# Narrow attention products filled to 128 rows of the array, with doubled low parts or zeros

## The chip, the cores and the metric

The kernel runs on one core of one Trainium2 chip. The metric is the device time of one execution in microseconds (us), the median of several runs. TensorE multiplies matrices, VectorE, ScalarE and GpSimd do the work by element, and one queue of SyncE (SP) issues all the DMAs of this kernel.

## The reference, cut to what matters

One inference step of a hybrid encoder trunk with two layers, all in 32-bit floats. A layer normalises its input, projects it, and runs three branches side by side: differential attention (DA: 4 heads, each with two maps of 64 features), a state-space scan (SSM), and stick-breaking attention (SB: 8 heads of 64 features). Their outputs are projected and added to the input, and a gated FFN with a short convolution follows.

```python
def diff_attn_block(q, k, v, q_pos, q_chunk, k_pos, k_chunk, rel_table, lam):
    ...
    s = jnp.einsum('bqhmd,bkhmd->bmhqk', q, k).astype(jnp.float32) * scale
    s = jnp.where(mask, s + bias[None, None].astype(jnp.float32), NEG_INF)
    p = jax.nn.softmax(s, axis=-1)
    p = p[:, 0] - lam * p[:, 1]
    return jnp.einsum('bhqk,bkhv->bqhv', p.astype(v.dtype), v)

def stick_breaking_block(q, k, v, q_pos, k_pos):
    z = jnp.einsum('bqhd,bkhd->bhqk', q, k).astype(jnp.float32) * (SB_HEAD_DIM ** -0.5)
    mask = k_pos[None, :] < q_pos[:, None]
    log_keep = jnp.where(mask, jax.nn.log_sigmoid(-z), 0.0)
    tail = lax.cumsum(log_keep, axis=3, reverse=True) - log_keep
    w = jnp.where(mask, jnp.exp(jax.nn.log_sigmoid(z) + tail), 0.0)
    return jnp.einsum('bhqk,bkhd->bqhd', w.astype(v.dtype), v)
```

There are 16 meta tokens and 512 prompt tokens in one sequence, and 8 sampled sequences of 16 new tokens that also attend to 512 cached ones each.

## The kernel before

All activations stand feature-major, with 656 columns: 16 meta, 512 prompt, 8 x 16 sampled (`NP` is 528). The dense products split each operand into a high part, rounded to the format fp32r, and a low part, the rest of it. A product is then three of fp32r, each one pass of TensorE; a product of whole 32-bit floats is two passes.

A layer runs SSM input and scan, then `da` for two pairs of heads (s = 0, 1), then `sb` for two groups of heads, and then the output projection `w_out` and the FFN. The in-projection of the next pair (`qkv_in`, issued with a priority offset of 400) and the parts of `w_out` that are ready are the dense work that TensorE does between the steps of an attention. The order of all instructions on each engine is fixed when the kernel is built, by a planner that simulates the engines and takes instructions by priority; the queues then run in that order.

The products that this case is about have fewer than 128 rows (the contracted index, on the partitions) because a head has 64 features, or because a block of keys has 16:

- `da_prompt`, scores. `stacked` puts the high part of a head's queries on the head's own 64 rows and the low part on the other 64 (`qs`), and the high part of its keys on both (`kd`). One product of 128 rows gives high by high plus low by high. The low part of the keys (`kl`) has only the head's own 64 rows, and a second product adds high by low from these:

```python
                    self.mm(ps, qs, kd[m][:, a:b], True, False)
                    self.mm(ps, qs[hs], kl[m][hs, a:b], False, True)
```

  The first block of queries (j = 0) doesn't use these, but whole floats on 64 rows (`qk,qk` in the profile).
- `sb_prompt`, scores: the same with keys and queries exchanged, `ks` by `qd` and then by `ql`.
- `da_prompt`, values. Prompt queries of block j see 128(j+1) + 16 keys. The weights are transposed by blocks of 128 keys (tile `pt`), the last 16 keys as a block of their own, and the product with these has 16 rows (`pv<-pt,vt 16*128`).
- `da_sample_values` and `sb_sample`: the new keys of four sampled sequences, 64 of them, are one half of the rows of `vt[:, 5]`; the product with the weights (`pts` or `nwt`) has 64 rows. In a DA group, products of 32 columns of the array (cached values, `kv` by `pts`) come right after it.

The tile `kv` holds 512 KB of cached keys or values, with four buffers in the pool of each branch.

Of the kernel before, what the change touches and what calls it, by code (L numbers as in the profile page):

```python
# [10 lines left out]
F32 = mybir.dt.float32  # L11
F32R = mybir.dt.float32r
# [6 lines left out]
# Columns of every feature-major tile: 16 meta tokens, 512 prompt tokens, then 8 sequences x 16 tokens.  # L19
# [15 lines left out]
# columns of the packed per-layer parameters  # L35
P_NM, P_NF, P_SUB, P_CW, P_CB, P_D, P_SN, P_FW, P_FB = 0, 8, 16, 17, 49, 57, 61, 65, 131
P_LQ, P_DTB, P_AL, P_N = 153, 157, 158, 159
# columns of the packed constants
# [3 lines left out]
class Bank:  # L42
    """Products that add into regions of one PSUM bank: the first clears its flags, the others are issued after it,
    so that each region starts from its first product."""
# [13 lines left out]
class Trunk:  # L58
# [33 lines left out]
    def act(self, out, in_, func, **kw):  # L92
        """ScalarE activation, the tables switched only between phases: all that use one set are issued before
        any of the next phase"""
        nc, tc = self.nc, self.tc
        mode = "silu_and_others" if func == AF.Silu else "natural_log_exp_and_others"
        nosync = mybir.DependencyInfo(mybir.DependencyClass.NoSync, mybir.DependencyReason.DATA)
        if mode != self.mode:
            self.gate = nc.scalar.preload_act_table_set(mode).ins
            for i in self.phase:  # L100
                tc.add_manual_dep(self.gate, i.name, nosync, reason="activation tables")
            self.mode, self.phase = mode, []
        i = nc.scalar.activation(out=out, in_=in_, func=func, **kw).ins  # L103
        tc.add_manual_dep(i, self.gate.name, nosync, reason="activation tables")
        self.phase.append(i)

    # ---------------------------------------------------------------- dense products
# [12 lines left out]
    def dense(self, wap, rhs, evac, cols=128, c0=0, w=None):  # L120
        """rhs: list of (hi, lo) tiles [128, T]; evac(columns, psum) reads the product of one half of them."""
# [18 lines left out]
    # ---------------------------------------------------------------- norms  # L140
    def x_first(self, g, pool):
        """x * g of the input and its norm"""
# [37 lines left out]
    def rstd_from(self, ss, n, out):  # L180
        """ss: sums of squares in PSUM, by half; out = (ss / n + eps) ** -0.5"""
# [5 lines left out]
    def ones_sum(self, *srcs, parts=None, tags=None):  # L187
        """sums over the partitions, on every partition, by half; with room for them, from the parts of src"""
# [19 lines left out]
    def scaled(self, out, scale=None):  # L208
        """evac writing psum * rstd (* scale) to out [*, T]"""
# [11 lines left out]
    def ext_evac(self, ext, hist):  # L221
        """evac writing psum * rstd with `hist` columns of room before the prompt and before each sequence"""
# [18 lines left out]
    def conv_silu(self, pool, ext, hist, wcol, bcol, out):  # L241
        """out[:, :T] = silu(depthwise causal conv of ext + b)"""
# [13 lines left out]
    # ---------------------------------------------------------------- the residual  # L256
# [5 lines left out]
    def x_load(self, src, pool=None, late=0):  # L262
        """the residual, in a pool of its own or in the room of the normalised one's high parts"""
# [8 lines left out]
    # ---------------------------------------------------------------- set-up  # L272
    def setup(self, ctx):
# [21 lines left out]
        # sums over the rows with the same place in blocks of 32  # L295
# [25 lines left out]
    def bias_tables(self, oneh, tab):  # L321
        """relative-position bias by (row, key) for the prompt, the sampled sequences and the meta rows"""
        nc, tc, D = self.nc, self.tc, self.D
        with tc.tile_pool(name="bp", bufs=1, reuse_waits="tile") as bp:
# [11 lines left out]
            # 128 copies of each head's row, so that a row's distance can differ from the next one's by one  # L336
# [23 lines left out]
    # ---------------------------------------------------------------- mixing-branch outputs  # L360
    def mix_pair(self, pool, tag, bufs):
        """two tiles of the output projection's operand"""
# [3 lines left out]
    def w_out(self, l, k0, pairs, nf_cols=None, offset=0, xpool=None):  # L366
        """x += the group's rows of the output projection; the last group moves x to xpool and prepares the FFN norm"""
# [27 lines left out]
    # ---------------------------------------------------------------- SSM branch  # L395
    def ssm_in(self, l, sp, spa):
# [7 lines left out]
        # dt rows  # L404
# [28 lines left out]
        # what is left of the decay to the end of each chunk  # L433
# [20 lines left out]
    def dt_in(self, l, pool, u):  # L454
        """the in-projection's tile of 8 columns, the parts of its weights side by side"""
# [27 lines left out]
    def ssd(self, l, sp, spb):  # L483
# [6 lines left out]
        for j, (t0, n) in enumerate(SCHUNK):  # L490
            sample = j == 5
            tsl = slice(t0, t0 + n)
            # token-major copies
# [7 lines left out]
            # C B^T, by group, sources on the partitions  # L501
# [70 lines left out]
            else:  # L572
                # the cached states' part: sequences on blocks of 32 rows, four at a time
# [34 lines left out]
                # what the sequences add to their states: two on each 32 rows, one of them masked  # L608
# [20 lines left out]
    def ssm_z(self, l, sp):  # L629
        """silu(z) = z / (1 + exp(-z)); the exponent is bounded where the quotient has long been 0"""  # L630
# [13 lines left out]
    def ssm_out(self, l):  # L644
        """gate, normalise per group; returns the two mix pairs"""
# [24 lines left out]
    # ---------------------------------------------------------------- attention inputs  # L670
    def qkv_in(self, l, v, outs_k, pool, offset=0):
        """four in_proj tiles, two of q (scaled) and two of k, and two more by token for the values"""
# [16 lines left out]
    def token_rstd(self):  # L689
        """the norm's factors by token: blocks of tokens on the partitions"""  # L690
# [6 lines left out]
        # 32 tokens from the last ones of the prompt  # L697
# [5 lines left out]
    def values(self, wap, vt):  # L703
        """two tiles of the in-projection, tokens on the partitions"""
        nc = self.nc
        w = [self.weights(wap[i], 4, 256, raw=True) for i in range(2)]
        for b0 in (4, 0, 2):
            ps = self.til(self.pmm, [128, 512], tag="mm")
            if b0 == 4:
                # the few tokens of block 4: four groups of products on blocks of 32 columns of the array  # L710
# [13 lines left out]
            with self.prio(-100):  # L724
                for b in (b0, b0 + 1):
                    if b == 4:
                        # the sums of the groups, until their own sum takes their place
# [13 lines left out]
    def q_blocks(self, pool, q, meta, tag):  # L741
        """queries as [128 (h2, d), (b, h2, t)], zero off the diagonal of h2"""
# [11 lines left out]
    # ---------------------------------------------------------------- differential attention  # L754
    def lam_cols(self, l, lam_init):
# [7 lines left out]
        # -(e1 - e2 + lam_init)  # L763
# [4 lines left out]
    def softmax_half(self, pool, rows, pss, tab, st, m):  # L768
        """exp(scores + bias - max) for map m, the scores in one or two pieces; the sums go to st"""
        nc = self.nc  # L770
        e = self.til(pool, [128, 576], tag="e", bufs=5)[:rows]
        c, mx = 0, BIG
# [10 lines left out]
        return e  # L783

    def softmax_mix(self, rows, es, st):
        """E0 / sum0 - lam E1 / sum1"""
# [7 lines left out]
    def stacked(self, pool, t, cols, tags, bufs, h, lo=None):  # L794
        """head h of a pair's tile t as operand parts on 128 rows: (high, low) on the head's own rows and on the
        others, or with `lo` (high, high), the low parts going to lo's rows of the head"""
# [7 lines left out]
        else:  # L804
            nc.gpsimd.tensor_copy(o[oth], t[own, cols])
            nc.vector.tensor_sub(lo[own], t[own, cols], o[own].bitcast(F32))
        return o

    def da_prompt(self, h, j, A, kd, kl, tb, oh, dap):
# [8 lines left out]
        for m in range(2):  # L818
# [3 lines left out]
            for a, b in zip(cuts, cuts[1:]):  # L822
                ps = self.sc()[:, : b - a]
                if j:
                    self.mm(ps, qs, kd[m][:, a:b], True, False)
                    self.mm(ps, qs[hs], kl[m][hs, a:b], False, True)
# [3 lines left out]
            es.append(self.softmax_half(dap, 128, pss, tab, st, m))  # L830
        p = self.softmax_mix(128, es, st)
        pt = self.til(dap, [128, 5, 128], tag="pt", bufs=3)
        ps = self.til(self.p1, [128, 512], tag="tp")
        for b in range(j + 1):
            self.tr(ps[:, 128 * b : 128 * b + 128], p[:, 128 * b : 128 * b + 128], 128)
        c0 = 128 * ((j + 1) % 4)
        pe = (ps if j < 3 else self.sc())[:16, c0 : c0 + 128]
        self.tr(pe, p[:, nk - 16 : nk], 128)
        nc.scalar.copy(pt[:16, j + 1, :], pe)
        nc.scalar.copy(pt[:, : j + 1, :].rearrange("p b c -> p (b c)"), ps[:, : 128 * (j + 1)])  # L840
        pv = self.til(self.p1, [128, 512], tag="pv")[:, :128]
        for b in range(j + 1):
            self.mm(pv, vt[:, b, 128 * h : 128 * h + 128], pt[:, b, :], b == 0, False)
        self.mm(pv, vt[:16, j + 1, 128 * h : 128 * h + 128], pt[:16, j + 1, :], False, True)
        nc.scalar.copy(oh[:, t0 : t0 + 128], pv)

    def da_sample_scores(self, l, s, g, m, A, qb, tb, st, dap):
        """rows (b, h2, t) of four sequences, map m: cached keys, then the 64 new ones"""
        nc = self.nc
        ps, pn = self.sc(), self.sc()[:, :64]  # L850
        for i2 in range(2):
            kt = self.til(dap, [128, 2, PAST], tag="kv", bufs=4)
# [14 lines left out]
    def da_sample_probs(self, g, p, dap):  # L867
# [8 lines left out]
        nc.vector.tensor_copy(pt[64 * g : 64 * g + 64, 4, :], pn)  # L876
        return pt

    def da_sample_values(self, l, s, g, A, pt, oh, dap):
        """values of four sequences: rows (b, h2, t), columns (h2, value)"""  # L880
        nc = self.nc
        rg = slice(64 * g, 64 * g + 64)
        pv = self.til(self.p1, [128, 512], tag="pv")[:, :256]
        bank = Bank(self)
        bank.mm(pv, pt[rg, 4, :], A["vt"][rg, 5, :])
        for j in range(4):
            vv = self.til(dap, [128, 4, 256], tag="kv", bufs=4)
# [14 lines left out]
    def da(self, l, s, A, dap, xpool):  # L902
# [6 lines left out]
        # meta rows  # L909
# [18 lines left out]
        # prompt rows of head g, with the sampled rows of four sequences  # L928
        es, st, pr = [None] * 2, [None] * 2, [None] * 2
        kl = [self.til(dap, [128, NP], F32R, tag="kl", bufs=2) for _ in range(2)]  # L930
        for u in range(8):
            h, j = u // 4, u % 4
            if u % 4 == 0:
                kd = [self.stacked(dap, k[m], slice(0, NP), ("kd", NP), 4, u // 4, kl[m]) for m in range(2)]
# [10 lines left out]
        # head norm  # L945
# [11 lines left out]
    # ---------------------------------------------------------------- stick-breaking attention  # L957
    def softplus(self, z, sp):
        """sp = softplus(z) for z in PSUM"""
# [6 lines left out]
    def sb(self, l, s, A, sbp, qk):  # L966
        """the results take the room of the pair's queries and keys in pool qk"""
# [4 lines left out]
        # sampled sequences: rows are (b, h2, t) of four sequences, columns (pair, four sequences, (h2, d))  # L972
# [7 lines left out]
    def sb_prompt(self, pr, A, pair, qk, sbp, sample):  # L980
        """two heads; weights by (key, query); the blocks of keys go from the last to the first"""
# [6 lines left out]
        # the last queries, zero off the diagonal of the heads  # L988
# [5 lines left out]
        ql = self.til(sbp, [128, NP], F32R, tag="ql", bufs=1)  # L994
        qd = [self.stacked(sbp, q, slice(0, NP), ("qd", NP), 4, h, ql) for h in range(2)]
# [445 lines left out]
```

## Time and profile before

| | us |
|---|---|
| median of 3 runs (2157.46 to 2159.97) | 2157.52 |
| span of the profiled execution | 2148.2 |
| what lies around the span, by the median | 9.3 |
| TensorE busy | 2115.9 |
| VectorE busy | 1323.8 |
| ScalarE busy | 876.7 |
| GpSimd busy | 296.6 |

The profile shows one execution, of which the span goes from the first to the last instruction; its own time is taken as the median, so that 9.3 us lie around the span. Matmuls are pipelined, and their recorded durations overlap: what a product costs is the distance from its start to the start of the next one. In the rows, `64*128 64x272` is a product with 64 rows and 128 columns of the array in use, that streams 272 columns; `PE` is TensorE, `DVE` VectorE, `ACT` ScalarE, `POOL` GpSimd, `SPq` the DMA queue. Line 87 is the helper through which nearly all products go, so tiles tell them apart.

### The profile page before, as it was taken

To read this page: it belongs to the slowest core of one execution; us is meant where nothing else is said; L and a number is where in the kernel's file an instruction comes from. 1 tells how busy PE (TensorE), PEld (TensorE's weight loads), DVE (VectorE), ACT (ScalarE), POOL (GpSimd) and SP (SyncE) were. 2 spreads that over 40 slices of the span, in tenths; PEclk is the share of its full clock that TensorE was granted. 3 is DMA by queue.
4 is the path that set the end of the run, shared out by engine and by line. 5 is a ranking of instruction groups with operands and counts; after the bars stand their busy time and mean duration, and the time that the engine had idled before them with its cause. 6 is when DMAs were issued, how large, how long until landed. Compare 5 with 4: busy or idle time off the path is not lost. (4 is left out here: it accounts for less than half of the span.)

```text
span 2148.2 us, 36738 instructions
## 1 busy us (share of the span) xinstructions
PE 2115.9 (98%) x14704; PEld 1937.8 (90%) x14704; DVE 1323.8 (62%) x2524; ACT 876.7 (41%) x1696; POOL 296.6 (14%) x586
## 2 busy tenths in 40 slices
PE   8999999999999999999999999999999999999998
PEld 6989888877899999999999888788778999999997
DVE  7897644677775544545468975547777655454544
ACT  3535444565542322223345354436555423132224
POOL 4241000222120000000123300002122100000002
PEclk9999999999999999999999999999999999999999
DMA  5535443453222222222324354336332222222222
GB/s 181 166 95 183 149 153 121 155 197 115 70 73 79 69 69 79 65 84 64 109 91 139 92 195 159 129 123 222 126 131 63 69 79 67 78 73 72 79 67 93
DMA packets 94500, 237.61 MB, mean 111 GB/s; under 512 B 12213, under 2 KB 31669, under 8 KB 94329
## 3 DMA queue, kind: packets, MB, share of 16 engines
q1 hardware_dynamic: 94328, 235.26, 34.5%
q8 instruction: 116, 1.90, 0.4%
q14 instruction: 56, 0.45, 0.1%
HBM read 212.06 MB, written 24.50 MB: 110 GB/s over the span
## 5 line engine op out<-in xcount | busy, mean ns | idle before, releaser
L87 PE MATMUL sc<-xh,whi 128*128 128x328 f32 (+1 forms) x1664 | 521.5, 314 | 3.8 <-ACT whi L115 3.4
L87 PE MATMUL sc<-xl,whi 128*128 128x328 f32 (+1 forms) x1664 | 520.7, 313 | 2.6 <-DVE xl L150 1.9
L87 PE MATMUL sc<-xh,wlo 128*128 128x328 f32 (+1 forms) x1664 | 518.7, 312 | 0.0
L115 ACT CAST whi<-wst 128x1024 fp32r<-128x1024 f32 (+2 forms) x241 | 237.9, 987 | 613.1 <-issue 310.6
L116 DVE TENSOR_TENSOR wlo<-wst,whi 128x1024 fp32r<-128x1024 f32 (+2 forms) x241 | 285.2, 1184 | 80.4 <-ACT whi L115 76.9
L87 PEld LDWEIGHTS sc<-xh,whi 128*128 128x128 f32 x1664 | 313.6, 189 | 5.7 <-ACT whi L115 4.6
L87 PEld LDWEIGHTS sc<-xl,whi 128*128 128x128 f32 x1664 | 314.3, 189 | 4.7 <-DVE xl L150 3.0
L87 PEld LDWEIGHTS sc<-xh,wlo 128*128 128x128 f32 x1664 | 314.6, 189 | 0.8 <-DVE wlo L116 0.4
L87 PE MATMUL mm<-xh,wlo 128*128 128x328 f32 x640 | 207.0, 323 | 0.0
L87 PE MATMUL mm<-xh,whi 128*128 128x328 f32 x640 | 205.0, 320 | 0.0
L87 PE MATMUL mm<-xl,whi 128*128 128x328 f32 x640 | 204.0, 319 | 0.0
L87 PE MATMUL sc<-ah,wlo 128*128 128x328 f32 (+2 forms) x634 | 197.4, 312 | 0.0
L87 PE MATMUL sc<-al,whi 128*128 128x328 f32 (+2 forms) x634 | 197.4, 311 | 0.0
L87 PE MATMUL sc<-ah,whi 128*128 128x328 f32 (+2 forms) x634 | 197.3, 311 | 0.0
L1200 DVE TENSOR_TENSOR x<-sc,x 128x328 f32<-128x328 f32 (+1 forms) x112 | 55.7, 497 | 147.4 <-PE sc L87 147.4
L87 PEld LDWEIGHTS mm<-xh,wlo 128*128 128x128 f32 x640 | 121.3, 190 | 9.8 <-issue 6.9
L87 PEld LDWEIGHTS mm<-xl,whi 128*128 128x128 f32 x640 | 121.3, 189 | 3.6 <-issue 2.2
L87 PEld LDWEIGHTS mm<-xh,whi 128*128 128x128 f32 x640 | 121.5, 190 | 2.9 <-issue 0.3
L87 PEld LDWEIGHTS sc<-al,whi 128*128 128x128 f32 x634 | 119.6, 189 | 0.0
L87 PEld LDWEIGHTS sc<-ah,whi 128*128 128x128 f32 x634 | 119.2, 188 | 0.0
L87 PEld LDWEIGHTS sc<-ah,wlo 128*128 128x128 f32 x634 | 119.2, 188 | 0.0
L1168 POOL COPY newf<-fext 128x2 f32<-128x2 f32 x44 | 8.1, 185 | 622.7 <-DVE fext L231 622.7
(364 smaller groups left out, 4042.9 us busy)
## 6 DMA issues: line engine op xcount, KB each, us to landing
wst<-win SPq DMA_DIRECT2D x56, 512.0 KB, 4.0
wst<-wg SPq DMA_DIRECT2D x44, 512.0 KB, 3.6
wst<-wu SPq DMA_DIRECT2D x44, 512.0 KB, 3.5
kv<-kda SPq DMA_DIRECT2D x32, 512.0 KB, 4.8
kv<-vda SPq DMA_DIRECT2D x32, 512.0 KB, 4.0
kv<-ksb SPq DMA_DIRECT2D x32, 512.0 KB, 4.4
kv<-vsb SPq DMA_DIRECT2D x32, 512.0 KB, 3.7
wst<-wout SPq DMA_DIRECT2D x24, 512.0 KB, 4.6
```

The lines of the kernel that those rows point to most:

```text
L87: self.nc.tensor.matmul(out, lhsT, rhs, start=start, stop=stop, **kw)
L115: nc.scalar.copy(hi, st)
L116: nc.vector.tensor_sub(lo, st, hi.bitcast(F32))
L1168: nc.gpsimd.tensor_copy(newf[:, f, :2], ext[:, NP : NP + 2])
L1200: nc.vector.tensor_add(xs, ps, xs)
```

## The change

- Scores of `da_prompt` and `sb_prompt`: the low part is copied by GpSimd to the other 64 rows as well, and the second product takes all 128 rows of both operands; it so adds low by low too. `kl` gets four buffers (two for each head) and `ql` two.
- Values of `da_prompt`: for j below 3 the weights of map 0 get 112 columns of zeros behind them, and the block of the last keys is transposed and multiplied as a full one. For j = 3 the block stays narrow in the transposition, and the rest of its rows in `pt` is zeroed.
- `da_sample_probs` zeroes the other half of the rows of `pts[:, 4]`, and `sb_new` keeps `nwt` once for each half with zeros on the other; both products take 128 rows.
- `kv` has three buffers instead of four.
- Comments are dropped all over the file.

```diff
@@ softmax_half
-    def softmax_half(self, pool, rows, pss, tab, st, m):
+    def softmax_half(self, pool, rows, pss, tab, st, m, pad=0):
         nc = self.nc
         e = self.til(pool, [128, 576], tag="e", bufs=5)[:rows]
-        c, mx = 0, BIG
+        c, mx = sum(ps.shape[1] for ps in pss), BIG
+        full = e[:, : c + pad]
+        if pad:
+            nc.gpsimd.memset(e[:, c : c + pad], 0.0)
+        c = 0
...
-        return e
+        return full
@@ stacked
             nc.vector.tensor_sub(lo[own], t[own, cols], o[own].bitcast(F32))
+            nc.gpsimd.tensor_copy(lo[oth], lo[own].bitcast(F32))
         return o
@@ da_prompt
-                    self.mm(ps, qs[hs], kl[m][hs, a:b], False, True)
+                    self.mm(ps, qs, kl[m][:, a:b], False, True)
...
-            es.append(self.softmax_half(dap, 128, pss, tab, st, m))
-        p = self.softmax_mix(128, es, st)
+            es.append(self.softmax_half(dap, 128, pss, tab, st, m, 0 if m or j == 3 else 112))
+        p = self.softmax_mix(128, [e[:, :nk] for e in es], st)
+        p = es[0]
         pt = self.til(dap, [128, 5, 128], tag="pt", bufs=3)
         ps = self.til(self.p1, [128, 512], tag="tp")
-        for b in range(j + 1):
+        n = min(j + 2, 4)
+        for b in range(n):
             self.tr(ps[:, 128 * b : 128 * b + 128], p[:, 128 * b : 128 * b + 128], 128)
-        c0 = 128 * ((j + 1) % 4)
-        pe = (ps if j < 3 else self.sc())[:16, c0 : c0 + 128]
-        self.tr(pe, p[:, nk - 16 : nk], 128)
-        nc.scalar.copy(pt[:16, j + 1, :], pe)
-        nc.scalar.copy(pt[:, : j + 1, :].rearrange("p b c -> p (b c)"), ps[:, : 128 * (j + 1)])
+        if j == 3:
+            nc.gpsimd.memset(pt[:, 4, :], 0.0)
+            pe = self.sc()[:16, :128]
+            self.tr(pe, p[:, 512:], 128)
+            nc.scalar.copy(pt[:16, 4, :], pe)
+        nc.scalar.copy(pt[:, :n, :].rearrange("p b c -> p (b c)"), ps[:, : 128 * n])
         pv = self.til(self.p1, [128, 512], tag="pv")[:, :128]
-        for b in range(j + 1):
-            self.mm(pv, vt[:, b, 128 * h : 128 * h + 128], pt[:, b, :], b == 0, False)
-        self.mm(pv, vt[:16, j + 1, 128 * h : 128 * h + 128], pt[:16, j + 1, :], False, True)
+        for b in range(j + 2):
+            self.mm(pv, vt[:, b, 128 * h : 128 * h + 128], pt[:, b, :], b == 0, b == j + 1)
@@ da_sample_scores, da_sample_values, sb_sample (each kv tile)
-            kt = self.til(dap, [128, 2, PAST], tag="kv", bufs=4)
+            kt = self.til(dap, [128, 2, PAST], tag="kv", bufs=3)
@@ da_sample_probs
         nc.vector.tensor_copy(pt[64 * g : 64 * g + 64, 4, :], pn)
+        nc.gpsimd.memset(pt[64 - 64 * g : 128 - 64 * g, 4, :], 0.0)
@@ da_sample_values
-        bank.mm(pv, pt[rg, 4, :], A["vt"][rg, 5, :])
+        bank.mm(pv, pt[:, 4, :], A["vt"][:, 5, :])
@@ da
-        kl = [self.til(dap, [128, NP], F32R, tag="kl", bufs=2) for _ in range(2)]
         for u in range(8):
             h, j = u // 4, u % 4
             if u % 4 == 0:
+                kl = [self.til(dap, [128, NP], F32R, tag="kl", bufs=4) for _ in range(2)]
@@ sb_prompt
-        ql = self.til(sbp, [128, NP], F32R, tag="ql", bufs=1)
-        qd = [self.stacked(sbp, q, slice(0, NP), ("qd", NP), 4, h, ql) for h in range(2)]
+        ql = [self.til(sbp, [128, NP], F32R, tag="ql", bufs=2) for _ in range(2)]
+        qd = [self.stacked(sbp, q, slice(0, NP), ("qd", NP), 4, h, ql[h]) for h in range(2)]
...
-                        self.mm(z[:, 0], ks[h0][hs[h0]], ql[hs[h0], t0 + a : t0 + e], False, a > 0)
+                        self.mm(z[:, 0], ks[h0], ql[h0][:, t0 + a : t0 + e], False, a > 0)
@@ sb_new
-        wt = self.til(sbp, [128, 2, 128], tag="nwt", bufs=1)
-        nc.scalar.copy(wt.rearrange("p r c -> p (r c)"), ps)
+        wt = self.til(sbp, [128, 2, 2, 128], tag="nwt", bufs=1)
+        nc.gpsimd.memset(wt, 0.0)
+        for g in range(2):
+            rg = slice(64 * g, 64 * g + 64)
+            nc.scalar.copy(wt[rg, g], ps[rg].rearrange("p (r c) -> p r c", c=128))
@@ sb_sample
-        bank.mm(pv[:, i, :], wt[rg, pr, :], A["vt"][rg, 5, 128 * pr : 128 * pr + 128])
+        bank.mm(pv[:, i, :], wt[:, g, pr], A["vt"][:, 5, 128 * pr : 128 * pr + 128])
```

## Rows read from the trace of the kernel before

**Rows 1.** The page: busy us by engine, and the granted clock in 40 slices.
```profile
PE 2115.9 (98%) x14704; PEld 1937.8 (90%) x14704; DVE 1323.8 (62%) x2524; ACT 876.7 (41%) x1696; POOL 296.6 (14%) x586
...
PEclk9999999999999999999999999999999999999999
```

**Rows 2.** Busy time by stretch: length, PE, PEld, DVE, ACT, POOL, clock, DMA, GB/s.
```profile
195.00:590.00 395.00, 395.00 (x2851) 322.31 (x2851) 251.67 (x607) 200.69 (x492) 47.42 (x102) 1.00 0.43 143
...
1250.00:1655.00 405.00, 405.00 (x2934) 331.91 (x2934) 260.99 (x627) 208.75 (x511) 51.13 (x113) 1.00 0.44 147
```

**Rows 3.** Waits of TensorE, longest group first: us in total, times, longest.
```profile
PE sc L87 <- DVE x L382: 6.0, 4, 1.7
```

**Rows 4.** Timeline of TensorE around one score: start us, duration us, instruction.
```profile
302.42 0.29 PE L87 MATMUL sc<-kd,qs 128*128 128x272 f32 x1
302.64 0.39 PE L87 MATMUL sc<-kl,qs 64*128 64x272 f32 x1
302.96 0.42 PE L87 MATMUL mm<-xh,wlo 128*128 128x328 f32 x1
303.21 0.31 PE L87 MATMUL mm<-xh,whi 128*128 128x328 f32 x1
303.36 0.31 PE L87 MATMUL mm<-xl,whi 128*128 128x328 f32 x1
```

**Rows 5.** Timeline of TensorE, products of parts on 128 rows.
```profile
567.13 0.28 PE L87 MATMUL sc<-sph,trir 128*128 128x264 f32 x1
567.25 0.29 PE L87 MATMUL sc<-spl,trir 128*128 128x264 f32 x1
567.38 0.39 PE L87 MATMUL sc<-S,negones 128*128 128x136 f32 x2
```

**Rows 6.** Counts and durations (by tile ns min/median/max; by line busy us, mean ns).
```profile
L87 PE MATMUL sc<-kl,qs x64: 382/388/452, 202.7 to 1416.9; 64*128 64x264 f32 x32, 64*128 64x272 f32 x16, 64*128 64x400 f32 x16
...
L87 PE MATMUL pv<-pt,vt 16*128 16x128 f32 x64 | 15.5, 321 | 0.0
...
L55 PE MATMUL pv<-vt,nwt 64*128 64x128 f32 x24 | 5.8, 323 | 0.0
...
L52 PE MATMUL pv<-vt,pts x16: 376/428/480, 242.7 to 1425.1; 64*128 64x256 f32 x16
```

**Rows 7.** Timeline of TensorE, values of prompt queries (full and 16-row passes merged).
```profile
259.81 0.80 PE L87 MATMUL pv<-pt,vt 128*128 128x128 f32 x4
260.54 0.55 PE L90 MATMUL tp<-con,e 128*128 128x128 f32 x3
...
360.07 1.02 PE L87 MATMUL pv<-pt,vt 128*128 128x128 f32 x6
361.03 0.28 PE L90 MATMUL sc<-con,e 128*16 128x128 f32 x1
```

**Rows 8.** Timeline of TensorE, values of sampled queries: new keys, then cached ones.
```profile
269.93 0.70 PE L52 MATMUL pv<-vt,pts 64*128 64x256 f32 x2
270.56 1.93 PE L55 MATMUL pv<-kv,pts 128*32 128x256 f32 x32
```

**Rows 9.** GpSimd's copies of the high part: ns min/median/max.
```profile
L805 POOL CAST kd<-qk x16: 619/1110/1553, 177.1 to 1323.9; 64x528 fp32r<-64x528 f32 x16
```

**Rows 10.** Loads of `kv`: time to landing, and one group in SP's timeline.
```profile
DMA to landing us min/median/max: 3.5/4.2/10.5
...
245.21 2.59 SPq L888 DMA_DIRECT2D kv<-vda  x4
```

**Rows 11.** Timeline of TensorE at the end of the attentions of layer 0.
```profile
580.96 2.05 PE L87 MATMUL tp<-W,vt 128*64 128x272 f32 x18
...
583.35 0.46 PE L87 MATMUL mm<-qk,whi 128*128 128x328 f32 x2
...
587.86 0.31 PE L87 MATMUL mm<-qk,wlo 128*128 128x328 f32 x1
```

**Rows 12.** VectorE's waits from 195 to 590 us, longest group first.
```profile
DVE e L776 <- PE sc L87: 16.2, 25, 2.3
```

More of the change, by code (lines that the diff above doesn't have):

```diff
@@ L881, in da_sample_values @@
         nc = self.nc
-        rg = slice(64 * g, 64 * g + 64)
         pv = self.til(self.p1, [128, 512], tag="pv")[:, :256]
         bank = Bank(self)
-        bank.mm(pv, pt[rg, 4, :], A["vt"][rg, 5, :])
+        bank.mm(pv, pt[:, 4, :], A["vt"][:, 5, :])
         for j in range(4):
-            vv = self.til(dap, [128, 4, 256], tag="kv", bufs=4)
+            vv = self.til(dap, [128, 4, 256], tag="kv", bufs=3)
             nc.sync.dma_start(vv, self.D["vda"][l, s, g, j])
@@ L1123, in sb_sample @@
         for i2 in range(2):
-            kt = self.til(sbp, [128, 2, PAST], tag="kv", bufs=4)
+            kt = self.til(sbp, [128, 2, PAST], tag="kv", bufs=3)
             nc.sync.dma_start(kt, D["ksb"][l, s, pr, g, :, 2 * i2 : 2 * i2 + 2, :])
@@ L1137, in sb_sample @@
         self.act(cs, cs, AF.Exp)
-        rg = slice(64 * g, 64 * g + 64)
-        bank.mm(pv[:, i, :], wt[rg, pr, :], A["vt"][rg, 5, 128 * pr : 128 * pr + 128])
+        bank.mm(pv[:, i, :], wt[:, g, pr], A["vt"][:, 5, 128 * pr : 128 * pr + 128])
         ps = self.til(self.p1, [128, 512], tag="tp")
@@ L1145, in sb_sample @@
         for b2 in range(2):
-            vc = self.til(sbp, [128, 2, 4, 128], tag="kv", bufs=4)
+            vc = self.til(sbp, [128, 2, 4, 128], tag="kv", bufs=3)
             nc.sync.dma_start(vc, D["vsb"][l, s, pr, g, b2])
```

## The prediction

> **What bounds the kernel now.** I read four views in turn. The page first: TensorE is busy for 98% of the span, VectorE for 62%, at a full granted clock [rows 1]. A busy TensorE need not be a useful one, so the next view is the busy time by stage. The four attentions of a layer lie at 195 to 590 us in layer 0 and at 1250 to 1655 us in layer 1; there TensorE is busy for every one of the 800 us, and VectorE for 252 of 395 and 261 of 405 [rows 2]. Third, the waits of TensorE: the longest group in the whole run is 6.0 us, and none of any size is one for attention operands [rows 3]. So whatever TensorE stops doing in these two stretches should come off the end, unless something else is then late.
>
> The fourth view, the timeline of TensorE, shows what it does there. Its recorded durations overlap, so one reads from start to start. Dense products of 328 columns start 0.15 us apart. The low-part product `kl,qs`, 272 columns on 64 rows, is different: the full product ahead of it holds TensorE from 302.42 to 302.64 (0.22 us), it itself until 302.96 (0.32), and the dense product behind it until 303.21 (0.25) [rows 4]. The same arithmetic on 128 rows, `sph,trir` and `spl,trir` with 264 columns, takes 0.12 and 0.13 us [rows 5]. Against 0.125, 0.125 and 0.15, the three steps are 0.095, 0.195 and 0.10 us too long: one narrow product between full ones costs 0.39 us beyond its stream, two changes of the used part of the array at some 0.195 each. I read it as a wait for the product ahead to leave (0.09) and a weight load that no longer lies beside the product ahead (0.10). The Trainium skill, TensorEngine Tiling (Array Packing), section Tiling Modes, says that changing the mode drains TensorE. By the drain alone the sum below would be about half (348 x 0.095 = 33 us); the step of the dense product behind, which no drain lengthens, speaks for the whole 0.39.
>
> **The change part by part.** Removed: excursions to 64 or 16 rows.
>
> *Scores.* `kl` has 64 such products [rows 6], `ql` in the stick-breaking branch the same 64 in the same shapes. They use one pass each and stand after a full product of the same score. 128 x 0.39 = 49.9 us. Walking along the timeline, 251 of the 256 changes have a full product on the other side and go; the other five border on another narrow product and stay (-1.0): 48.9.
>
> *Probabilities times values, the last 16 keys.* Products of whole floats take two passes. A run of four passes (two full, two on 16 rows) holds TensorE from 259.81 to 260.54, 0.73 us, and a run of six (four full) from 360.07 to 361.03, 0.96 [rows 7]. Two more full passes are thus some 0.22 us, 0.11 each, and the 16-row run costs 0.73 - 0.44 = 0.29 too much; the product behind it pays between 0.05 and 0.10 (0.10 is the dense product's [rows 4]; the three transposes from 260.54 show less). I take 0.35. There are 64 passes, 32 products [rows 6]: 11.2 us.
>
> *New keys of the sampled sequences.* `nwt` has 16 products of two passes (24 of the 32 passes in the row shown), with the mean of the 16-row ones, 323 ns against 321 [rows 6]; at 0.35 that is 5.6 us, less 5 of 32 changes that border on 32-column products: 4.6. `pts` has 8 products (16 passes); the two passes hold TensorE from 269.93 to 270.56, 0.63 against four times 0.11 (256 columns, two passes), but what follows uses 32 columns [rows 6, 8], so only one change of the two goes: 8 x 0.195 = 1.6.
>
> Sum removed: 48.9 + 11.2 + 4.6 + 1.6 = 66.3 us. Upper bound, all 360 conceivable changes at 0.195: 70. Lower, 0.17 for each of the 348 that I counted: 59.
>
> Added on TensorE: streams have the same columns, so filling rows adds none. 24 transposes of 16 columns become 128 wide; between 0 and one pass of 0.11 each (2.6 us). I take 0, since the moving operand, the identity, has 128 columns both times.
>
> Added elsewhere: 32 copies of the low part to the other 64 rows, on GpSimd, behind VectorE's subtraction. The like copy of the high part takes 0.62 to 1.55 us [rows 9], so 20 to 50 us on an engine that is busy for 47 of 395 us [rows 2]. It is first needed by the second block of queries (the first uses `qk` directly) or, in the other branch, after two blocks of keys; meanwhile TensorE has dense products, as around the score shown [rows 4]. Taken at 0; were that cover gone, 16 first uses in the differential branch x 1.55 = 25 us. The zero fills are smaller and on GpSimd too; ScalarE loses a small copy per block of queries. Taken at 0, and at most a microsecond or two either way.
>
> `kv` has three buffers instead of four. A 512 KB load lands after a median of 4.2 us, and the four loads of `vda` issued together at 245.21 to 247.8 are used from 270.56 on, 23 us later [rows 8, 10]. With three, the fourth of each such group can only be issued when the first has been used: eight groups x 4.2 = 34 us of lateness for TensorE's products of sampled values, with dense work to fill them. The loads share SP's one queue with the weights (`wst`) behind them, which are then late by as much. Taken at 0 where there is filler.
>
> At the end of a stretch there is little: behind the last value products of layer 0, from 580.96 on, the previous output projection still gives 18 products between 583.35 and 587.86, 2.7 us of dense work [rows 11]. I charge 3 us for each layer, 6 in all.
>
> Sum: -66.3 + 6 = -60.3. The profiled span is 2148.2 us, the median of the runs 2157.5, so 9.3 lie around it. 2148.2 - 60.3 + 9.3 = 2097.
>
> **The rivals.**
> *A: the attentions keep their length.* If the chain through VectorE and ScalarE sets the length of a stretch, TensorE uses up its dense work early and idles at the end. Price: 33 us per layer saved, less 2.7 of filler, so 30 of idle each; gain 6, time 2151; half of it, 2124. For it: VectorE is 64% busy and little filler is left [rows 2, 11]. Against: VectorE's longest waits in the stretch are for TensorE (16.2 us for scores alone) [rows 12], so the chain shortens too when scores come sooner.
> *B: slower, by three `kv` buffers.* The 128 loads (32 of each of four kinds) would each have to hold TensorE for 0.52 us to eat 66 us; that is where it decides. Fully exposed, at 4.2 us, they would cost 538. At 0.65 each: 2157.5 - 66 + 83 = 2174. Against it: loads issued 23 us ahead. For it: SP's order, in which weights stand behind a load that waits for its buffer.
> *C: the narrow products are free now.* If they ran beside their neighbours on the other rows, filling them would add their streams: 128 x 0.13 + 96 passes x 0.11 + 16 x 0.22 = 31 us, so 2189. The Trainium skill, TensorE: Matmul & The Clock Gate, Part 3, says that products on distinct groups of rows run at once, some 4 ns apart. Here the product behind `kl` starts 0.32 us later, so the trace disagrees for this order.
> *D: rows are not the cause.* If the lost time came from two products adding into one bank, nothing would change: 2157 to 2163. Against: `sph` and `spl` add into one bank at 0.12 [rows 5].
>
> **How the numbers follow.** Forecast (2080 to 2112): 0.76. A, between 2112 and 2152: 0.13; B 0.05; C 0.02; D 0.04, of which 0.03 within 4.3 us (0.2%, about what the measurement can tell) and 0.01 slower. Faster: 0.76 + 0.13 = 0.89 and 0.02 of B's milder half = 0.91; same 0.03; slower 0.03 + 0.02 + 0.01 = 0.06. The order of work is written by a planner and will be new; 373 changes to 32 columns and the like remain, at 0.195 some 73 us, and a tenth more or less of them is 7. Low end: 2157.5 - 70 - 7 = 2080. High end: half of A, 2124. Outside lie half of A, B, C and D, under 2 in 10.
>
> **What would show it.** Right: `kl,qs` and `ql,ks` on 128 rows with 0.12 to 0.18 us from start to start, like their neighbours; `pt,vt` in even steps of 0.11; TensorE's busy time in the two stretches lower by some 33 us each, with the FFN stretches unchanged. A shows as TensorE waiting for VectorE or ScalarE shortly before the FFN, B as TensorE waiting for a `kv` DMA or for ScalarE's weight copies. The forecast is wrong if the steps stay at 0.32 with 128 rows, or if they fall and new waits of more than 10 us stand in the stretches.

## The result and the profile after

The changed kernel takes 2129.61 us (median of 4 runs, 2129.04 to 2139.68) beside 2158.70 for the kernel before in the same comparison: a ratio of 0.9879, with an interval of [0.9855, 0.9903]. It is faster, but by a good deal less than was forecast (2097, range 2080 to 2124).

One thing is needed to read the numbers below: runs of one and the same kernel lie on levels some 8.6 us apart (the kernel before near 2149 or, as in all four of its runs above, near 2158, so that one such step is in the 29.1 us between the medians; the cause is in the last section), so a difference between two kernels is taken here between their lowest runs or between profiled spans, and the ratio stands beside it. On that footing the change is worth -19.6 us (2129.04 against 2148.66, the lowest run of the kernel before beside e1 to e4 below), and -21.0 by the spans (2127.2 against 2148.2). The prediction set 9.3 us around the profiled span. The changed kernel's profiled execution has 2129.04 - 2127.2 = 1.8 there, and so has that lowest run of the kernel before (2148.66, span 2146.9). With 1.8 the forecast would have read 2089.7; its difference, -60.3, stays as it is.

The page of the kernel after, busy us by engine:

```profile
PE 2080.1 (98%) x14704; PEld 1930.9 (91%) x14704; DVE 1314.6 (62%) x2524; ACT 876.0 (41%) x1676; POOL 345.0 (16%) x662
```

Busy time by stretch, kernel after (columns as in [rows 2]: length, PE, PEld, DVE, ACT, POOL, granted clock, DMA share, GB/s). The first two lines are the stretches of [rows 2]; then, for layer 0, differential attention (first score to last value product), what lies between, stick-breaking attention (first score in parts to last value product); then 10 us near its end:

```profile
195.00:590.00 395.00, 384.18 (x2881) 324.60 (x2880) 254.81 (x611) 204.43 (x486) 68.82 (x138) 0.99 0.43 144
1250.00:1655.00 405.00, 394.29 (x2982) 335.83 (x2981) 268.17 (x622) 213.70 (x496) 79.92 (x154) 1.00 0.43 143
...
201.70:390.50 188.80, 188.59 (x1417) 164.73 (x1417) 102.52 (x287) 80.08 (x196) 11.21 (x29) 1.00 0.47 157
390.50:423.70 33.20, 30.51 (x208) 26.51 (x207) 20.40 (x39) 16.51 (x34) 7.78 (x19) 1.00 0.64 229
423.70:580.20 156.50, 148.58 (x1143) 118.01 (x1141) 120.34 (x258) 97.87 (x238) 46.04 (x85) 0.97 0.38 122
...
565.00:575.00 10.00, 8.51 (x56) 6.79 (x56) 6.15 (x14) 5.83 (x16) 0.61 (x1) 0.52 0.01 2
```

The same view of the kernel before, cut at the same events:

```profile
202.40:383.40 181.00, 181.00 (x1260) 148.82 (x1260) 98.31 (x281) 79.14 (x206) 4.61 (x8) 1.00 0.44 148
383.40:411.10 27.70, 27.70 (x191) 23.37 (x190) 19.08 (x37) 13.97 (x28) 6.00 (x16) 1.00 0.60 198
411.10:582.80 171.70, 171.70 (x1294) 136.63 (x1295) 125.72 (x263) 100.63 (x242) 36.81 (x78) 1.00 0.40 134
```

In these stretches, where TensorE was never idle before, it now idles some 11 us in a layer, 7.9 of them in stick-breaking attention, and near the end of that the granted clock is down to half. More telling is the first stretch: differential attention got *longer*, 188.8 us for 181.0, though many of its products are now cheaper, and TensorE is busy through it with more instructions (1417 for 1260). Stick-breaking attention's first score in parts comes 12.6 us later, and its stretch is shorter.

TensorE's timeline of the kernel after (start, recorded duration) has both halves of the story:

```profile
302.93 0.28 PE L87 MATMUL sc<-kd,qs 128*128 128x272 f32 x1
303.05 0.29 PE L87 MATMUL sc<-kl,qs 128*128 128x272 f32 x1
303.18 0.31 PE L87 MATMUL mm<-xh,wlo 128*128 128x328 f32 x1
303.33 0.31 PE L87 MATMUL mm<-xh,whi 128*128 128x328 f32 x1
...
362.70 0.83 PE L87 MATMUL pv<-pt,vt 128*128 128x128 f32 x6
363.29 0.40 PE L87 MATMUL mm<-xl,whi 128*128 128x328 f32 x1
...
366.68 0.59 PE L52 MATMUL pv<-vt,pts 128*128 128x256 f32 x2
367.21 1.50 PE L55 MATMUL pv<-kv,pts 128*32 128x256 f32 x24
...
373.34 0.64 PE L55 MATMUL pv<-kv,pts 128*32 128x256 f32 x8
...
385.08 1.05 PE L87 MATMUL pv<-pt,vt 128*128 128x128 f32 x8
...
389.47 1.28 PE L87 MATMUL pv<-pt,vt 128*128 128x128 f32 x10
```

The same group of sampled values, and the prompt values behind it, on TensorE's timeline of the kernel before:

```profile
362.25 0.70 PE L52 MATMUL pv<-vt,pts 64*128 64x256 f32 x2
362.87 1.93 PE L55 MATMUL pv<-kv,pts 128*32 128x256 f32 x32
...
376.49 1.24 PE L87 MATMUL pv<-pt,vt 128*128 128x128 f32 x8
...
382.21 1.47 PE L87 MATMUL pv<-pt,vt 128*128 128x128 f32 x10
```

The score's three steps are 0.12, 0.13 and 0.15 us where [rows 4] had 0.22, 0.32 and 0.25, and six passes of prompt values take 0.59, 0.10 each: the operands do what was forecast. But the sampled values, 32 passes in one run before, come as 24 and, 6.1 us later, 8. SP's timeline tells why. The kernel after, and then the kernel before:

```profile
346.85 0.69 SPq L897 DMA_DIRECT2D kv<-vda  x1
367.91 0.33 SPq L897 DMA_DIRECT2D kv<-vda  x1
```

```profile
342.50 1.76 SPq L888 DMA_DIRECT2D kv<-vda  x4
```

Before, the four loads of this group go out together 20 us ahead of their use at 362.87. After, the fourth goes out at 367.91, just behind the start of the products (367.21) that free its buffer. TensorE's waits (total, times, longest) hardly show it:

```profile
PE mm L87 <- DVE xh L382: 4.4, 7, 1.2
...
PE sc L87 <- ACT sph L137: 3.0, 4, 1.5
...
PE pv L55 <- DMA kv<-vda: 0.2, 1, 0.2
```

TensorE waits 0.2 us for a `kv` load in the whole run: in the order that the planner fixed, other products stand between the 24 passes and the 8.

### The profile page after: what moved, and what is told of

Its sections match the earlier page's. It is cut to its first block, busy times and chain, and to the rows that moved or that the text cites. A ratio compares the mean times of both kernels' runs of the same rounds, so it can differ in the third digit from the quotient of the medians.

```text
span 2127.2 us, 36809 instructions
## 1 busy us (share of the span) xinstructions
PE 2080.1 (98%) x14704; PEld 1930.9 (91%) x14704; DVE 1314.6 (62%) x2524; ACT 876.0 (41%) x1676; POOL 345.0 (16%) x662
## 4 chain that ended last, share of the span: by engine, by line
PE 90%; DVE 5%; ACT 1%; issue 1%; POOL 1%; DMA 1%; SPq 0%; DVEq 0%; ACTq 0%; POOLq 0%
PE sc L87 58%; PE mm L87 25%; PE tp L87 2%; PE pv L55 2%; PE tp L90 2%; PE pv L87 1%; DVE M L526 1%; POOL sq L156 1%; ACT W L103 0%; DVE wlo L116 0%; DVE xl L170 0%; DMA kv<-vda 0%; PE pv L52 0%; DVE y L1260 0%; DVE sps L1146 0%
```

## The experiments

All compute the full reference. "Lowest" is the difference of the lowest run from the lowest of the kernel before (2148.66); DA is the length of differential attention in a layer (the two layers agree within 0.2 us), idle the whole run's idle time of TensorE, changes the changes of the used part of the array counted along its timeline (a transposition of softmax weights counts as a full product).

| kernel | ratio | lowest, us | DA, us | idle, us | changes |
|---|---|---|---|---|---|
| before | 1 | 0 | 181.0 | 20.6 | 721 |
| after | 0.9879 [0.9855, 0.9903] | -19.6 | 188.8 | 35.6 | 407 |
| e1_da_kv4 | 0.9815 [0.9787, 0.9843] | -39.7 | 167.0 | 28.5 | 386 |
| e2_da_only | 0.9838 [0.9809, 0.9868] | -35.7 | 167.0 | 16.8 | 533 |
| e3_sb_only | 0.9914 [0.9881, 0.9946] | -16.2 | 181.0 | 20.9 | 578 |
| e4_kv3 | 1.0194 [1.0156, 1.0232] | +40.5 | 206.7 | 34.7 | 744 |
| e5_kv3_da | 1.0117 [1.0084, 1.0149] | +23.5 | 206.7 | 27.3 | 751 |
| e6_kv3_sb | 1.0017 [0.9998, 1.0036] | +1.4 | 181.0 | 18.9 | 724 |
| e7_parts | 0.9728 [0.9699, 0.9757] | -59.8 | 163.0 | 18.1 | 398 |
| e8_parts_nwt | 0.9712 [0.9683, 0.9740] | -63.7 | 163.0 | 17.8 | 376 |
| e9_after_sc | 0.9832 [0.9812, 0.9852] | -33.7 | 170.4 | 28.6 | 416 |
| e10_kv3_sc | 1.0041 [1.0027, 1.0055] | +10.9 | 190.1 | 16.9 | 761 |
| e11_parts_sb3 | 0.9769 [0.9719, 0.9818] | -47.3 | 163.0 | 22.2 | 386 |
| e12_parts_kv3 | 0.9897 [0.9852, 0.9942] | -20.6 | 188.7 | 34.4 | 420 |

### The suspected cost alone, and parts of the change

The main test puts three `kv` buffers into the kernel before and changes nothing else:

```diff
-            kt = self.til(dap, [128, 2, PAST], tag="kv", bufs=4)
+            kt = self.til(dap, [128, 2, PAST], tag="kv", bufs=3)
```

and so for each of the four `kv` tiles (e4), for the two of differential attention (e5), for the two of stick-breaking attention (e6).

> The kernel before with three kv buffers in both branches and nothing else. Theory K: the late fourth loads and the split groups of cached products cost 8 to 16 us, 2166 to 2175, with the last prompt products of the differential branch later. Theory C: TensorE still has dense work to fill, so 2157 to 2162.

> The kernel before with three kv buffers in the differential branch alone. With three in both branches the time rose by 1.9%, some 41 us. Theory K (groups of four loads in the differential branch): most of it is here, 25 to 35 us more than before, with the last prompt products of the first pair of layers some 20 us later (403 to 408 us instead of 383). Rival, the stick-breaking branch is where it hurts: 0 to 12 us more.

> The kernel before with three kv buffers in the stick-breaking branch alone. Filling that branch with three buffers brought 18 us where the steps had promised 29, so theory K expects 8 to 14 us more than before. Rival, the missing 11 us were the chain of that branch: 0 to 4 us more.

Measured: +40.5, +23.5 and +1.4 us. The buffer alone costs as much as is missing from the forecast (-60.3 + 40.5 = -19.8; the change gave -19.6). That it fits to 0.2 us is chance, for the price depends on the kernel that it is taken from (43.1 in e12 below). The expectations had the size wrong: 8 to 16 us for e4, 25 to 35 for e5, 8 to 14 for e6, whose rival (0 to 4) came true. Two alone don't add up to both (24.9 against 40.5); why is not settled. Windows of e4, differential attention, then 171.6 us behind it:

```profile
202.00:408.40 206.40, 206.22 (x1416) 168.75 (x1415) 101.71 (x287) 80.81 (x207) 5.38 (x8) 1.00 0.45 143
408.40:580.00 171.60, 165.28 (x1183) 130.13 (x1182) 126.44 (x266) 100.08 (x234) 37.20 (x84) 1.00 0.44 146
```

Differential attention is stretched by 25.7 us a layer. TensorE stays busy in the first window, with 156 instructions more than the kernel before had in its own: dense work that is then missing behind.

The other way round, e1 gives the changed kernel four buffers in differential attention only (`kl` goes back to two so that they fit on chip), e2 fills only differential attention, with four buffers everywhere, and e3 is the kernel before with stick-breaking attention's part of the change, its three buffers included:

The edit of e1 (both `kv` tiles), and of e2 besides it, against the changed kernel; then that of e3 against the kernel before:

```diff
-            kt = self.til(dap, [128, 2, PAST], tag="kv", bufs=3)
+            kt = self.til(dap, [128, 2, PAST], tag="kv", bufs=4)
-                kl = [self.til(dap, [128, NP], F32R, tag="kl", bufs=4) for _ in range(2)]
+                kl = [self.til(dap, [128, NP], F32R, tag="kl", bufs=2) for _ in range(2)]
```

```diff
-        ql = [self.til(sbp, [128, NP], F32R, tag="ql", bufs=2) for _ in range(2)]
+        ql = self.til(sbp, [128, NP], F32R, tag="ql", bufs=1)
...
-                        self.mm(z[:, 0], ks[h0], ql[h0][:, t0 + a : t0 + e], False, a > 0)
+                        self.mm(z[:, 0], ks[h0][hs[h0]], ql[hs[h0], t0 + a : t0 + e], False, a > 0)
...
-            kt = self.til(sbp, [128, 2, PAST], tag="kv", bufs=3)
+            kt = self.til(sbp, [128, 2, PAST], tag="kv", bufs=4)
```

```diff
-                        self.mm(z[:, 0], ks[h0][hs[h0]], ql[hs[h0], t0 + a : t0 + e], False, a > 0)
+                        self.mm(z[:, 0], ks[h0], ql[h0][:, t0 + a : t0 + e], False, a > 0)
...
-            kt = self.til(sbp, [128, 2, PAST], tag="kv", bufs=4)
+            kt = self.til(sbp, [128, 2, PAST], tag="kv", bufs=3)
...
-        bank.mm(pv[:, i, :], wt[rg, pr, :], A["vt"][rg, 5, 128 * pr : 128 * pr + 128])
+        bank.mm(pv[:, i, :], wt[:, g, pr], A["vt"][:, 5, 128 * pr : 128 * pr + 128])
```

> The changed kernel with four kv buffers again in the differential branch (two kl buffers instead of four make the room), three still in the stick-breaking branch. Theory K (the fourth load of a group of four cached values comes too late and holds the last query blocks of the differential branch): the last prompt products of the second pair in layer 0 lie near 382 us instead of 389.5, the stick-breaking branch starts some 7 us earlier in each layer, and the time falls from 2129.6 to 2110 to 2118. Theory C (only the stick-breaking chain sets the length, whatever happens ahead of it): its first products start at the same time, and the time is 2126 to 2132.

> Only the differential branch filled to 128 rows (scores, last keys, sampled new keys), four kv buffers in both branches, the stick-breaking branch as before. By the sum of the steps the removed changes of the array are worth 24.4 + 11.2 + 1.6 = 37 us, so 2158.7 - 37 = 2122 if nothing is lost; theory K expects that, 2119 to 2127, because no buffer is taken away. Theory C expects half of it, 2136 to 2145, because the stick-breaking branch would run out of dense work.

> Only the stick-breaking branch filled to 128 rows (low parts of the queries and the new keys), with three kv buffers there, the differential branch as before with four. By the sum of the steps 24.5 + 4.6 = 29 us less, 2130, if nothing is lost. Theory C, in which this branch's own chain has a fixed length: 2145 to 2156, with TensorE idle near the end of the branch. Theory K for this branch (three buffers hurt here too): between the two, with waits for kv loads.

With four buffers differential attention falls to 167.0 us, 14 less than before and 22 less than in the changed kernel, and the time by 20.1 us. So neither VectorE's chain nor the copies on GpSimd had kept it long. e1 is still 8 us of idle above the kernel before, with three buffers left in stick-breaking attention. Filling differential attention alone (e2) brings 35.7 of the 37 us that its steps promised, stick-breaking attention alone with three buffers (e3) 16.2 of 29.

### The filling without the cost

Four buffers in both branches don't fit beside the doubled low parts. The same products can be had with smaller operands: the stacked tile carries (high, low) of the side that is kept (`kd`, `qd`), and the side made anew for each block gives (high, high) and (low, low), 128 columns each. The four terms are the same.

```diff
-                qs = self.stacked(dap, q[m], slice(t0, t0 + 128), ("qs", 128), 6, h)
+                ql = self.til(dap, [128, 128], F32R, tag="ql", bufs=6)
+                qs = self.stacked(dap, q[m], slice(t0, t0 + 128), ("qs", 128), 6, h, ql)
...
-                    self.mm(ps, qs, kl[m][:, a:b], False, True)
+                    self.mm(ps, ql, kd[m][:, a:b], False, True)
...
-                        self.mm(z[:, 0], ks[h0], ql[h0][:, t0 + a : t0 + e], False, a > 0)
+                        self.mm(z[:, 0], kl[h0], qd[h0][:, t0 + a : t0 + e], False, a > 0)
```

e7 has this with four `kv` buffers and `nwt` as before, e8 `nwt` filled too, and three buffers instead of four for the small tiles of stick-breaking attention. e11 and e12 are e8 with three `kv` buffers (the line shown for e4) in stick-breaking attention and in both.

> All scores on 128 rows with four kv buffers in both branches: the keys of the differential branch and the queries of the stick-breaking one carry (high, low) on the two halves of the rows, and the small operand has two tiles of 128 columns, (high, high) and (low, low), so that the long doubled low parts go and make the room. The last 16 keys and the sampled new keys of the differential branch are filled as in the changed kernel, the new keys of the stick-breaking branch as before. Theory K: the whole 49 + 11 + 1.6 = 62 us, a ratio of 0.971, some 2090. Theory C (the stick-breaking chain sets its stretch, buffers or not): 2105 to 2112 as with four buffers in the differential branch alone.

> The same, with the new keys of the stick-breaking branch filled too; three buffers instead of four for the tiles of 128 columns there make the room. Theory K: 4.6 us below the one without, 0.969, some 2086, if the small tiles are not missed; Theory C: no less than the one without.

> The version with (high, high) and (low, low) small tiles and the new keys filled, but three kv buffers in the stick-breaking branch. Between the changed kernel with four buffers in the differential branch only (0.9815) and this version with four in both (0.9712) lie 22 us, and two things differ: the buffers of this branch and the operands. Theory K (the buffers of the stick-breaking branch cost more once its steps are shorter and dense work is scarce): 10 to 20 us are lost again, a ratio of 0.976 to 0.981. Rival (the long doubled low parts and their copies cost it): 0.971 to 0.974.

> The same with three kv buffers in both branches, so that it differs from the changed kernel by the operands alone. Theory K: the differential branch of a layer grows from 163 us by some 20 again, and the ratio is 0.984 to 0.990, as the changed kernel's 0.9879. Rival (the operands made the difference): 0.975 to 0.980.

e8 is the best kernel of the study: its lowest run, 2084.98 us, is 63.7 below that of the kernel before, its median, 2090.20, 60.6 below the other's in their comparison. Its score steps on TensorE's timeline are the changed kernel's:

```profile
202.31 0.29 PE L87 MATMUL sc<-kd,ql 128*128 128x272 f32 x1
202.44 0.29 PE L87 MATMUL sc<-kd,qs 128*128 128x272 f32 x1
202.56 0.29 PE L87 MATMUL sc<-kd,ql 128*128 128x272 f32 x1
202.69 0.32 PE L87 MATMUL mm<-xh,whi 128*128 128x328 f32 x1
```

and its windows have no idle TensorE in differential attention nor in the 34.9 us behind it:

```profile
202.20:365.10 162.90, 162.90 (x1259) 144.60 (x1259) 95.77 (x281) 78.18 (x193) 16.86 (x57) 1.00 0.50 165
365.10:400.00 34.90, 34.90 (x250) 29.39 (x249) 23.88 (x51) 19.79 (x44) 9.89 (x31) 1.00 0.52 176
```

Taking the buffer out of it (e12) gives back 43.1 us and lands on the changed kernel: lowest run 2128.10 against 2129.04, DA 188.7 against 188.8. So which operands carry the parts hardly matters; the buffer does. In stick-breaking attention alone it costs 16.4 here (e11) where it cost 1.4 in the kernel before (e6), and the step from there to both 26.7.

### By what a late load makes an attention longer

Sampled values add into the tile `pv`, of which there is one; the prompt's next values need the same tile. In e9 (the changed kernel) and e10 (the kernel before with three buffers in differential attention) they add into one of the score banks:

```diff
-        pv = self.til(self.p1, [128, 512], tag="pv")[:, :256]
+        pv = self.sc()[:, :256]
```

> The changed kernel, three kv buffers, but the sampled values of the differential branch add up in one of the four score banks instead of the one value bank that the prompt's values use too. Theory P (the late fourth load keeps the single value bank, and the prompt's next query blocks wait for that bank): the differential branch of a layer shrinks from 188.8 us towards the 167 that four buffers gave, and the time comes to 2112 to 2120. Rival S (the loads themselves or the order of products set it, whatever the bank): 185 to 195 us and 2125 to 2135.

> The kernel before with three kv buffers in the differential branch, and the sampled values there in a score bank. Theory P: the branch comes back from 206.7 us to some 181, and the time is within 8 us of the kernel before. Rival S: 200 to 210 us and 20 to 30 us above before.

Differential attention falls from 188.8 to 170.4 us in e9, where four buffers gave 167.0, and from 206.7 to 190.1 in e10, where they gave 181.0. Most of the lengthening, 18.4 of 21.8 and 16.6 of 25.7 us, thus goes with the one tile. The loads do not come sooner there: from the new keys' product to the last cached pass, the eight groups of sampled values hold their bank for 72.7 us in e9 and 93.9 in e10, where they held `pv` for 59.2 in the changed kernel and 25.4 in the kernel before. e10 still misses what was expected of it, some 181 us and a time within 8 us of before. TensorE's timeline, last prompt values of layer 0, in e4 and then in e10:

```profile
402.42 1.24 PE L87 MATMUL pv<-pt,vt 128*128 128x128 f32 x8
407.15 1.47 PE L87 MATMUL pv<-pt,vt 128*128 128x128 f32 x10
```

```profile
385.85 1.25 PE L87 MATMUL pv<-pt,vt 128*128 128x128 f32 x8
391.29 1.47 PE L87 MATMUL pv<-pt,vt 128*128 128x128 f32 x10
```

e9 comes 14.1 us below the changed kernel, of the 20.1 that e1 wins with the buffer itself. The rest was not followed further. Neither kernel was run with the score bank and four buffers.

## Why the prediction was right in sign and wrong in size

**Right: TensorE is the bound, and changes cost.** "... whatever TensorE stops doing in these two stretches should come off the end, unless something else is then late": e8 shows the first half of it. It has 345 changes fewer than before and a span shorter by 64.0 us, of which 2.8 is idle time; (64.0 - 2.8) / 345 = 0.177 us for a change, if all the rest is theirs, beside the 0.195 of the sum and its lower bound of 0.17. From start to start along TensorE's timeline, before and after in the changed kernel, the terms are: `kl,qs` and `ql,ks` together 42.5 to 19.5 us and `kd` and `qd` ahead of them 35.3 to 22.8, so 35.5 for the 128 pairs where 128 x (0.095 + 0.195) = 37.1 were taken; prompt values 34.2 to 24.1, against 11.2 taken off with the step behind; `nwt` 6.6 to 4.1, against 4.6 with the step behind. The rest stands in the steps of the products behind, which were not added up. The Trainium skill, TensorEngine Tiling (Array Packing), section Tiling Modes, says that a change of the mode drains the array. The drain alone had been put at 33 us for all of it by estimate, and the 61.2 measured in e8 say that the step behind belongs to the price as well.

**Right as far as seen: no cost on GpSimd.** It is busy for 345.0 us instead of 296.6, and no wait of TensorE in the changed kernel names `kl` or `ql`. The wider transposes cost nothing, as was taken: in 14 places the last one of a block of queries starts 0.109 us after the one ahead, a dense product 0.028 behind it and the next dense product 0.234 behind that (medians), with 16 columns before and with 128 after.

**Not needed, and near by luck: the end of a stretch.** 6 us were charged for idle TensorE. With the filling alone (e8) idle time fell by 2.8. That e8's 64.0 still lie near the 60.3 of the sum is in part luck: the changes gave 61.2 of the 66.3 taken for them, and the charge made up for that.

**Wrong: "`kv` has three buffers instead of four. ... Taken at 0 where there is filler."** This is the step that failed. The lateness was read rightly: the fourth load of each of the eight groups goes out when the first ones are used, and lands some 3.5 us later. The price was then looked for in one place only, TensorE standing still for that load, and filler does cover that (0.2 us in all). Three things were left out. First, what the late product *holds*: between `vt,pts` and the last cached pass the `pv` tile is taken for 2.6 us before (362.25 to 364.80) and 7.3 after (366.68 to 373.98), over the eight groups 25.4 and 59.2, and the prompt's next values queue behind it: 385.08 and 389.47 in the changed kernel, 376.49 and 382.21 before. Second, filler is not free: TensorE is 98% busy with a fixed amount of dense work, and what covers differential attention is missing behind it, where the 11 us of idle a layer stand. In layer 0 the last product of the dense work in [rows 11] (`mm<-qk`) is at 538.06 instead of 587.86, before an attention that runs to 580. The idle time of the whole run rises from 20.6 to 35.6 us, and the granted clock falls to 1.2 GHz there. Third, cached scores of four sequences are 8 passes of 32 columns of the array, which run four at a time, their starts 7 ns apart, when their loads are there together; half a group holds TensorE about as long. One of each on the timeline of the kernel before, and of the kernel after:

```profile
207.03 1.06 PE L87 MATMUL sc<-kv,qb 128*32 128x512 f32 x8
```

```profile
205.33 1.05 PE L87 MATMUL sc<-kv,qb 128*32 128x512 f32 x4
```

Before, 25 of 42 groups are of eight passes and 5 of four; after, 17 and 26 of 49, and all 256 passes take 47.0 us instead of 38.9.

How the 43.0 us between the spans of e8 and the changed kernel divide: idle 17.8; half-speed clock for 10.2 us at 565 and 3.4 at 1616, of which TensorE is busy for 12.0 and loses half, 6.0; cached scores 47.0 - 40.1 = 6.9; 31 changes more, 14 of them at the 7 further groups of cached scores and so counted already, the other 17 at 0.177: 3. That is some 34; the other 9 are not assigned.

**The rivals.** *B* had the right cause and the wrong path: it priced the buffers as TensorE waiting for them, asked for 0.52 us a load to decide, and got a chance of 0.05 with a time of 2174. The cost is 43.1 / 128 = 0.34 us a load, below the point where it decides the sign, and far from the zero in the forecast; nothing in the range stood for a half-priced B. Its announced signs hardly showed: TensorE waits 0.2 us for a `kv` load, and 4.0 for ScalarE's weight copies, where it was 3.4 before. *A* gives the time that came (2112 to 2152), and some of its picture: idle TensorE before the FFN, and from the first score to the last value product of layer 0 still 378.5 us (201.70 to 580.20) where it was 380.4. Its mechanism fell with e1 and e8: with four buffers the attention does shorten, by 14 and 18 us in differential attention. *C* and *D* are refuted by the steps of 0.12 and 0.13.

## What to carry to other kernels

When a change pays with a buffer, price the buffer by itself, best by taking it out of the old kernel: e4's one-number edit showed 40 of the 60 us going. A late load under a busy engine need not show as a wait; follow what its consumer holds (here an accumulation tile) and who needs that next, and count the filler as borrowed from the stretch that comes after. And products that leave half of the rows unused between full ones are worth filling, if the operands are chosen so that the filling costs no buffer.

## What the runs showed of the hardware

The steps of 8.6 us come from TensorE's clock in the state-space stretch, where VectorE is the busy engine and TensorE has gaps. Around 143 and 1200 us (1174 to 1227) the granted clock drops to half, 1.2 GHz, in every profile; in the kernel before TensorE stands idle for 2.2 us up to 142.5, and the drop is at 143.7. In most profiles the clock is back after 6.8 us, in three (e5, e6 and e9) one or both drops last 23.9. The window of 150 to 160 us (columns as above) in e6, and that of 140 to 160 in the kernel before, from which e6 differs only in the buffers of stick-breaking attention:

```profile
150.00:160.00 10.00, 10.00 (x41) 8.45 (x39) 6.05 (x16) 0.00 (x0) 0.00 (x0) 0.50 0.36 133
```

```profile
140.00:150.00 10.00, 7.53 (x41) 5.37 (x39) 10.00 (x13) 2.25 (x3) 8.88 (x6) 0.69 0.18 52
150.00:160.00 10.00, 10.00 (x66) 8.28 (x65) 9.41 (x25) 0.07 (x1) 0.00 (x0) 0.97 0.48 179
```

A long drop loses (23.9 - 6.8) / 2 = 8.6 us; e6's profiled run had two and took 2166.69 us, 16.7 above its lowest. The mean granted clock of a whole run goes with it: for the kernel before 0.995 at 2148.66 us, 0.991 at 2157.93, 0.986 at 2168.08. What makes a drop long in one execution and short in the next wasn't tried.
